# Moving a weight pool to the other end of SBUF, with the operand tiles below it, and splitting the recurrence scores into quarters

## The chip, the cores and the metric

One core of one Trainium2 chip runs the whole program. The metric is device time in microseconds (us) of one execution, lower is better. The median of three timed runs of the kernel before is 2441.2 us (2435.44 to 2445.77).

## What is computed

The input is 256 tokens of width 2048, float32. Three layers follow each other, and nearly all arithmetic is in dense products of those 256 tokens with weight matrices that are read once:

```python
# first block
u = rms_norm(h, mix_pre_g)
q, k, v, ca, cb, ga, gb = split(u @ w_in)                 # 2048 -> 9216
y_attn = neighbourhood_attention(q, k, v, rpb) @ w_attn_o
y_conv = conformer_conv(ca, cb, w_dw, b_dw, ln_g, ln_b, w_conv_o)
h = h + rms_norm((sigmoid(ga) * y_attn + sigmoid(gb) * y_conv) @ w_out, mix_post_g)
gate, up = split(rms_norm(h, ffn_pre_g) @ w_gate_up)      # 2048 -> 2 x 5632
h = h + rms_norm((silu(gate) * up) @ w_down, ffn_post_g)  # 5632 -> 2048
# second block, even layer
q, k, v, g_a, u, g_b = split(x @ w_in)                    # 2048 -> 6144
x = layer_norm(alpha * x + concat(stick_breaking(q, k, v) * silu(g_a), pool(u) * silu(g_b)) @ w_out)
# second block, odd layer: 32 heads of 64, products w_r w_k w_v w_g, two small lora products, and per head
sa = state @ (-kk_t)
state = state * w_t + sa * (kk_t * a_t) + v_t * k_t
o_t = state @ r_t
x = layer_norm(alpha * x + (norm(o) + bonus) * silu(g) @ w_o)
```

The recurrence is not stepped token by token. The kernel takes chunks of 64 tokens, and its scores are products within a chunk between two rows of keys, receptances and their decays ("gram" below).

## The kernel before

**Products.** Every float32 operand is kept as a high part and a remainder, both in the fp32r type, and a product is the sum of three matmuls: high by high, high by remainder, remainder by high. A weight piece of 256 rows by 512 columns is one DMA of 512 KB on SP's queue (`split_w`, L146) into `wraw`; ScalarE (ACT) copies it to `wh` (L149), VectorE (DVE) subtracts to get `wl` (L151). Four pieces of each are held in the pool "wts".

There are two forms of product. `ws` (weight-stationary, L168 to L170) loads a 128 by 128 block of the weights into TensorE (PE) and streams the 256 tokens of `x` past it; it serves outputs that are wanted with features on the partitions. `ts` (token-major, L187 to L189) loads a 128 by 128 block of `x` and streams 512 weight columns past it. In the trace's names the moving operand stands first: `acc<-xk,wh` is `ws`, `acc<-wh,xk` is `ts`. The `x` of a product lies in one of four kinds of tile: `xk` (a ring of 16 tiles, by far the most), `slab` (the mixer: attention output and convolution output, for w_attn_o and w_conv_o), `f` (the 44 row blocks of the gated FFN, for w_down), and `evm` (the merged tensor of the even layer, for its w_out). `xpool` tiles of the even layer share the `evm` slots and go through `ws`-like lines L846 to L848; the odd layer's small lora products are L1029 to L1031 and L1045 to L1047, with their weights `lh`, `ll` stationary and `lm`, `lx` moving.

**What sets the order.** Each engine runs its own list in order. PE's list interleaves the products with "background" pieces: `tick()` is called after each weight piece and releases one piece of queued work (transposes, attention heads, the recurrence). A tile pool hands out addresses when it is opened, from the bottom of SBUF upwards by default, and a pool closed gives them back.

**Start.** `mixer` calls `ahead(first_tile, 6, 0, ...)`: six blocks of 128 features (`x_piece`, 256 features each, L306) are read, transposed on PE (L246), scaled and split into `xk` (ACT L316, DVE L317) before the first product; the other ten come from the background. SP's queue takes the pieces in the order x0 w0 x1 w1 x2 w2 x3 x4 w3. ACT's first activation instruction needs a table load, which is placed ahead of it in ACT's list.

**Recurrence.** 16 units (4 groups of heads by 4 chunks) each run `gram` (L1360): per pair p, two matmuls, one on the upper 64 partitions of the operands and one on the lower 64, each with all 128 columns stationary and 128 moving, both float32 (each shows as two records, so 16 records a unit). `gmask` then zeroes what a score must not see, and later steps read 64-column parts of the result G.

Of the kernel before, what the change touches and what calls it, by code (L numbers as in the profile page):

```python
# [8 lines left out]
F32 = mybir.dt.float32  # L9
F32R = mybir.dt.float32r  # L10
# [27 lines left out]
class Mega:  # L38
    def __init__(self, ctx, tc, a, out):
        self.ctx, self.tc, self.nc, self.a, self.out = ctx, tc, tc.nc, a, out  # L40
        self.bg, self.loads, self.ready = [], deque(), deque()
        self.barrier = None
        self.cp = ctx.enter_context(tc.tile_pool(name="const", bufs=1))
        self.wp = ctx.enter_context(tc.tile_pool(name="wts", bufs=1))
        self.split_pool, self.depth = (self.wp, 4), 3
        self.xp = ctx.enter_context(tc.tile_pool(name="ring", bufs=16))
        self.sp = ctx.enter_context(tc.tile_pool(name="small", bufs=2))
        self.c1 = ExitStack()
        self.sp1 = self.c1.enter_context(tc.tile_pool(name="small1", bufs=1))
        self.pacc = ctx.enter_context(tc.tile_pool(name="pacc", bufs=4, space=bass.MemoryType.PSUM))  # L50
        self.paux = ctx.enter_context(tc.tile_pool(name="paux", bufs=4, space=bass.MemoryType.PSUM))
# [102 lines left out]

    def ws(self, W, col0, X, evac):

        nc = self.nc
        kt = self.a[W].shape[1] // P
        ps = [self.acc() for _ in range(4)]
        for k0 in range(0, kt, 2):  # L160
            wh, wl = self.next_w(W, col0, k0)
            for n in range(4):
                c = slice(n * P, n * P + P)
                o = ps[n][:, :T]
                for kk in range(2):
                    k = k0 + kk
                    x = X[k]
                    nc.tensor.matmul(o, wh[:, kk, c], x[:, 0], start=k == 0, stop=False)  # L168
                    nc.tensor.matmul(o, wh[:, kk, c], x[:, 1], start=False, stop=False)  # L169
                    nc.tensor.matmul(o, wl[:, kk, c], x[:, 0], start=False, stop=k == kt - 1)  # L170
                if k0 + 2 == kt:
                    evac(n, o)
            self.tick()
# [92 lines left out]
    def constants(self):  # L266
        nc, cp, a = self.nc, self.cp, self.a
        self.ident = cp.tile([P, P], F32, name="ident")
        nc.gpsimd.memset(self.ident, 1.0)
        nc.gpsimd.affine_select(out=self.ident, in_=self.ident, pattern=[[-1, P]], channel_multiplier=1,  # L270
                                base=0, compare_op=ALU.is_equal, fill=0.0)
        self.ones = cp.tile([P, P], F32, name="ones")
        nc.gpsimd.memset(self.ones, 1.0)
        self.mhalf = cp.tile([P, 16], F32, name="mhalf")
        nc.gpsimd.memset(self.mhalf, -0.5)

        src = a["vecs"]
        nblk = src.shape[0] // P
        self.vec = cp.tile([P, nblk * P], F32, name="vec")
        st = self.sp1.tile([P, nblk, P], F32, name="vst")  # L280

        def turn(b):
            ps = self.aux()
            nc.tensor.transpose(ps[:, :P], st[:, b], self.ident)
            nc.vector.tensor_copy(self.vec[:, b * P:b * P + P], ps[:, :P])

        def load():
            with self.tc.issue_after(self.paced[1].ins):
                nc.scalar.dma_start(out=st[:, 1:], in_=src[P:].rearrange("(b r) p -> r b p", r=P))

        nc.scalar.dma_start(out=st[:, 0], in_=src[0:P])
        turn(0)

        self.later = [load] + 4 * [lambda: None] + [lambda b=b: turn(b) for b in range(1, nblk)]
# [60 lines left out]
    def mixer(self):  # L355
        nc, a = self.nc, self.a
        ctx = ExitStack()
        pp = ctx.enter_context(self.tc.tile_pool(name="mix", bufs=1))
        W = "w_in"

        def slab(shape, dt=F32):
            return pp.tile(shape, dt, tag="slab", name="slab", bufs=6)

# [4 lines left out]
                self.x_piece(k // 2)  # L370

        def first_tile(k):
            if k % 2 == 0 and k < 6:
                self.x_piece(k // 2)
            x = self.to_fm(k, "mix_pre_g")
            if k % 2 and k < 6:
                with self.tc.issue_after(self.turned.ins):
                    self.fetch_w(k // 2 + 1)
            return x
        X = self.ahead(first_tile, 6, 0, fetch=piece)  # L380
        norm = {}

        def squares(c):
# [256 lines left out]
    def ffn(self, X, parts):  # L640
        nc, a = self.nc, self.a
        ctx = ExitStack()
        pp = ctx.enter_context(self.tc.tile_pool(name="ffn", bufs=1))
        W = "w_gate_up"
        r = self.rpow(self.ssq_total(parts), 2, 1.0 / D, 1e-6)
# [3 lines left out]
        def turn(gt):  # L649
# [12 lines left out]
            def halves(m):  # L662
                def go():
                    ps = st[m].rearrange("p (n t) -> p n t", n=2)
                    f = pp.tile([P, 2, 2, T], F32R, tag="f", name="f", bufs=FT // 2)
                    nc.scalar.activation(out=f[:, :, 0], in_=ps, func=AF.Copy)
                    nc.vector.tensor_tensor(out=f[:, :, 1], in0=ps, in1=f[:, :, 0].bitcast(F32), op=ALU.subtract)
                    F.extend(f[:, n] for n in range(2))
                return go
# [47 lines left out]
    def even(self, X):  # L717
        nc, a = self.nc, self.a
        ctx = ExitStack()
        pp = ctx.enter_context(self.tc.tile_pool(name="even", bufs=1))  # L720
        W = "ev_w_in_2"
        scale = 128.0 ** -0.5
# [75 lines left out]
        def pool_group(g):  # L798
# [13 lines left out]
            def means():  # L812
                for n in range(2):
                    d = pp.tile([P, T], F32, tag="pd", name="pd", bufs=2)
                    nc.vector.tensor_tensor(out=d, in0=st["sum"][:, n, 16:], in1=icnt[:, g], op=ALU.mult)
                    nc.vector.tensor_tensor(out=d, in0=d, in1=up[:, 2 * g + n, 16:], op=ALU.subtract)
                    x = pp.tile([P, 2, T], F32R, tag="evm", name="xpool", bufs=8)
                    self.split(x, d)
                    pooled[2 * g + n] = x
            return sums, means  # L820
# [37 lines left out]
        for i in range(2):  # L858
            def ev_ga(n, ps, i=i):
                t = pp.tile([P, T], F32, tag="gt", name="gt", bufs=2)  # L860
                nc.scalar.activation(out=t, in_=ps, func=AF.Silu)
                nc.vector.tensor_tensor(out=t, in0=t, in1=oa[:, 4 * i + n], op=ALU.mult)
                x = pp.tile([P, 2, T], F32R, tag="evm", name="evm", bufs=8)
                self.split(x, t)
                M[4 * i + n] = x
            self.ws(W, 3072 + 512 * i, X, ev_ga)
# [26 lines left out]
    def odd(self, normed):  # L893
# [411 lines left out]
        def bank(n=CH):  # L1305
            return self.aux()[:, :4 * n].rearrange("p (u s) -> p u s", s=n)
# [16 lines left out]
        def unit(j, c):  # L1323
# [31 lines left out]
            def gram():  # L1355
                ar, bk, G = st["ar"], st["bk"], st["G"]
                pss = [bank(P) for _ in HALF]
                for p in range(4):
                    for h2, hs in enumerate(HALF):
                        nc.tensor.matmul(pss[h2][:, p], bk[hs, p], ar[hs, p], start=True, stop=True)  # L1360
                for h2, ps in enumerate(pss):
                    nc.vector.tensor_tensor(out=G[:, h2], in0=ps, op=ALU.mult,
                                            in1=gmask[:, h2].unsqueeze(1).broadcast_to((P, 4, P)))
# [366 lines left out]
```

## Time and profile before

| | us |
|---|---|
| median of 3 runs | 2441.2 |
| the profiled execution's own time | 2436.61 |
| its span on the core | 2434.8 |
| PE busy within the span | 2372.7 |
| DVE busy | 1515.6 |
| ACT busy | 1214.4 |
| POOL busy | 223.4 |

The profiled execution lies 4.6 us under the median. Its time holds 1.8 us outside the span. The mean granted clock of TensorE is 0.991 of full speed. A PE matmul is pipelined: the "us" or "mean ns" of one reaches from its start to its modelled end and overlaps the next one, so what a stream of matmuls costs is read from the distance between starts (the pitch), either from two starts with the number of matmuls between them, or from the number of matmuls in a window that holds nothing else.

### The profile page before, as it was taken

What the parts mean: (1) busy time and instruction counts of PE and PEld (TensorE: products, weight loads), DVE (VectorE), ACT (ScalarE), POOL (GpSimd) and SP (SyncE); (2) the same over time, 40 slices, a digit from 0 to 9 for tenths busy, and PEclk for the clock granted to TensorE, in tenths of its full rate; (3) what the DMA queues carried; (4) which work ended last, traced back from release to release, by engine and by line L of the source; (5) the groups of instructions that cost most, each with busy time, mean ns of one, the idle gap of its engine ahead of it and who ended that gap; (6) DMA issues with size and microseconds to landing.
All of it is one profiled execution on the core that took longest, in us unless ns stands there. A gap on an engine that the chain in (4) does not pass through costs nothing.

```text
span 2434.8 us, 39170 instructions
## 1 busy us (share of the span) xinstructions
PE 2372.7 (97%) x15385; PEld 2072.3 (85%) x15385; DVE 1515.6 (62%) x2093; ACT 1214.4 (50%) x1937; POOL 223.4 (9%) x343
## 2 busy tenths in 40 slices
PE   8999999999999999999999999999999998999997
PEld 8998888788788888888888898999889996789975
DVE  5688888565654454454444544555587678885656
ACT  5433564444544444444344444564387765455662
POOL 0000200100000000000000000320000013145411
PEclk9999999999999999999999999999999999999998
DMA  7666656556566666666666556455666688866665
GB/s 230 196 185 192 175 170 189 160 185 203 160 191 190 190 190 185 191 191 190 193 194 191 168 184 190 149 164 182 196 189 194 185 238 232 220 169 157 149 169 135
DMA packets 287912, 451.18 MB, mean 185 GB/s; under 512 B 57903, under 2 KB 85103, under 8 KB 287727
## 3 DMA queue, kind: packets, MB, share of 16 engines
q1 hardware_dynamic: 263488, 428.50, 59.9%
q10 hardware_dynamic: 21167, 11.79, 1.8%
q0 software_dynamic: 3072, 8.39, 1.6%
q8 instruction: 121, 1.98, 0.3%
q14 instruction: 64, 0.52, 0.1%
HBM read 428.74 MB, written 17.77 MB: 183 GB/s over the span
## 4 chain that ended last, share of the span: by engine, by line
PE 78%; issue 7%; DVE 6%; DMA 4%; ACT 3%; POOL 1%; SPq 0%; ACTq 0%; DVEq 0%; POOLq 0%
PE acc L187 17%; PE acc L188 17%; PE acc L189 17%; PE acc L168 7%; PE acc L169 7%; PE acc L170 7%; DVE wl L151 2%; DMA wraw<-in_od_w_v 1%; ACT wh L149 1%; DMA wraw<-in_od_w_g 1%; DMA wraw<-in_od_w_k 0%; DMA inv<-md 0%; PE aux L246 0%; PE aux L659 0%; DVE xk L65 0%
## 5 line engine op out<-in xcount | busy, mean ns | idle before, releaser
L151 DVE TENSOR_TENSOR wl<-wraw,wh 128x1024 fp32r<-128x1024 f32 x762 | 935.1, 1228 | 752.8 <-ACT wh L149 750.0
L149 ACT ACTIVATE wh<-wraw 128x1024 fp32r<-128x1024 f32 x762 | 805.9, 1058 | 1004.4 <-PE acc L189 644.6
L187 PE MATMUL acc<-wh,xk 128*128 128x512 f32 x1520 | 599.6, 395 | 1.8 <-ACT kr L1226 1.3
L188 PE MATMUL acc<-wl,xk 128*128 128x512 f32 x1520 | 595.2, 392 | 5.4 <-DVE wl L151 5.3
L189 PE MATMUL acc<-wh,xk 128*128 128x512 f32 x1520 | 594.9, 391 | 0.0
L168 PE MATMUL acc<-xk,wh 128*128 128x256 f32 x1920 | 550.3, 288 | 0.5 <-ACT rr L1069 0.5
L169 PE MATMUL acc<-xk,wh 128*128 128x256 f32 x1920 | 544.5, 284 | 0.0
L170 PE MATMUL acc<-xk,wl 128*128 128x256 f32 x1920 | 540.8, 284 | 0.6 <-DVE wl L151 0.6
L168 PEld LDWEIGHTS acc<-xk,wh 128*128 128x128 f32 x1920 | 369.4, 193 | 4.4 <-ACT rr L1069 0.9
L169 PEld LDWEIGHTS acc<-xk,wh 128*128 128x128 f32 x1920 | 370.0, 193 | 0.4
L170 PEld LDWEIGHTS acc<-xk,wl 128*128 128x128 f32 x1920 | 367.5, 192 | 1.6 <-DVE wl L151 1.2
L188 PEld LDWEIGHTS acc<-wl,xk 128*128 128x128 f32 x1520 | 286.0, 188 | 65.3 <-DVE wl L151 7.5
L187 PEld LDWEIGHTS acc<-wh,xk 128*128 128x128 f32 x1520 | 285.9, 188 | 61.4 <-ACT kr L1226 1.5
L189 PEld LDWEIGHTS acc<-wh,xk 128*128 128x128 f32 x1520 | 286.1, 188 | 59.6
L187 PE MATMUL acc<-wh,f 128*128 128x512 f32 x352 | 139.1, 395 | 0.0
L188 PE MATMUL acc<-wl,f 128*128 128x512 f32 x352 | 138.9, 395 | 0.0
L189 PE MATMUL acc<-wh,f 128*128 128x512 f32 x352 | 138.9, 395 | 0.0
L427 DVE SCALAR_TENSOR_TENSOR slab<-zp,vec,slab 128x256 f32<-128x256 f32 x240 | 117.9, 491 | 4.2
L189 PEld LDWEIGHTS acc<-wh,f 128*128 128x128 f32 x352 | 66.3, 188 | 15.5
L187 PEld LDWEIGHTS acc<-wh,f 128*128 128x128 f32 x352 | 66.3, 188 | 15.5
L188 PEld LDWEIGHTS acc<-wl,f 128*128 128x128 f32 x352 | 66.3, 188 | 15.3
L725 POOL TENSOR_SCALAR_AFFINE_SELECT tri<-ones 128x128 f32<-128x128 f32 x1 | 0.3, 294 | 727.0 <-ACT junk L235 727.0
(318 smaller groups left out, 2149.1 us busy)
## 6 DMA issues: line engine op xcount, KB each, us to landing
wraw<-in_w_gate_up SPq DMA_DIRECT2D x176, 512.0 KB, 3.6
wraw<-in_w_in SPq DMA_DIRECT2D x144, 512.0 KB, 4.3
wraw<-in_ev_w_in SPq DMA_DIRECT2D x96, 512.0 KB, 3.6
wraw<-in_w_down SPq DMA_DIRECT2D x88, 512.0 KB, 4.7
wraw<-in_w_out SPq DMA_DIRECT2D x32, 512.0 KB, 4.2
wraw<-in_ev_w_out SPq DMA_DIRECT2D x32, 512.0 KB, 4.8
wraw<-in_od_w_r SPq DMA_DIRECT2D x32, 512.0 KB, 4.7
wraw<-in_od_w_k SPq DMA_DIRECT2D x32, 512.0 KB, 4.6
```

Of the source, the lines that this page charges most:

```text
L149: high = nc.scalar.activation(out=wh, in_=raw, func=AF.Copy)
L151: low = nc.vector.tensor_tensor(out=wl, in0=raw, in1=wh.bitcast(F32), op=ALU.subtract)
L168: nc.tensor.matmul(o, wh[:, kk, c], x[:, 0], start=k == 0, stop=False)
L169: nc.tensor.matmul(o, wh[:, kk, c], x[:, 1], start=False, stop=False)
L170: nc.tensor.matmul(o, wl[:, kk, c], x[:, 0], start=False, stop=k == kt - 1)
L187: nc.tensor.matmul(ps[t], x[:, 0, c], wh[:, kk], start=k == k1, stop=False)
L188: nc.tensor.matmul(ps[t], x[:, 0, c], wl[:, kk], start=False, stop=False)
L189: mm = nc.tensor.matmul(ps[t], x[:, 1, c], wh[:, kk], start=False, stop=k == k2 - 1)
L427: nc.vector.scalar_tensor_tensor(out=zc[:, n], in0=src, scalar=self.v1("w_dw", j * 8 + n), in1=zc[:, n], op0=ALU.mult, op1=ALU.add)
L725: nc.gpsimd.affine_select(out=tri, in_=self.ones, pattern=[[-1, P]], channel_multiplier=1, base=0, compare_op=ALU.is_ge, fill=0.0)
```

## The change

It has four parts.

1. **Pools.** The weight pool "wts" is opened at the right-hand side (the upper end) of SBUF. The slots of `slab`, `f` and of `evm` with `xpool` get pools of their own, "slabs", "gated" and "merged", opened first in their stage and so directly above the ring and the small pools, which themselves slide down by the size of the weight pool. Bytes per partition as both programs are built:

| tiles | before | after |
|---|---|---|
| weights (wraw, wh, wl) | 36544 to 85696 | 180192 to 229344 |
| xk ring | 85696 to 118464 | 36544 to 69312 |
| slab | 146176 to 195328 | 81792 to 130944 |
| f (22 tiles of 4096) | 139072 to 229184 | 81792 to 171904 |
| evm and xpool | 198464 to 214848 | 75072 to 91456 |
| lora weights lh | 186336 and up | between 133824 and 172048 |

   By the remainder of the start address modulo 256: weights and xk both 192 before, 224 and 192 after; f and evm 64, slab 0 before; f and slab 128, evm 64 after. In the last product of the kernel before (w_o), the second half of the weights lies at 182976 and up, remainder 192, moving past stationary xk.

2. **Start.** A small activation "warm" on a constant stands ahead of all others on ACT. Only four blocks are made before the first product; the transposes of the blocks after the fourth are placed behind the last product matmul written so far. SP's order becomes x0 w0 x1 w1 x2 w2 x3 w3 x4.

3. **Scores.** Each of gram's matmuls becomes two, with 64 stationary columns each; the four quarters of a pair go in the order (0,0), (1,1), (0,1), (1,0) of (row half, column half). 16 matmuls a unit in place of 8, with the same output.

4. **What moves along.** Other addresses decide which tile waits for which, so the scheduler's order differs at the border of FFN and even layer and within the recurrence; elsewhere the lists agree up to line numbers.

```diff
-        self.wp = ctx.enter_context(tc.tile_pool(name="wts", bufs=1))
+        self.wp = ctx.enter_context(tc.tile_pool(name="wts", bufs=1, side="right"))
...
-                    nc.tensor.matmul(o, wl[:, kk, c], x[:, 0], start=False, stop=k == kt - 1)
+                    self.mm = nc.tensor.matmul(o, wl[:, kk, c], x[:, 0], start=False, stop=k == kt - 1)
...
+        nc.scalar.activation(out=self.sp1.tile([P, 16], F32, name="warm"), in_=self.mhalf, func=AF.Copy)
...
+        lower = ctx.enter_context(self.tc.tile_pool(name="slabs", bufs=6))
         pp = ctx.enter_context(self.tc.tile_pool(name="mix", bufs=1))
...
-            return pp.tile(shape, dt, tag="slab", name="slab", bufs=6)
+            return lower.tile(shape, dt, tag="slab", name="slab")
...
         def first_tile(k):
-            if k % 2 == 0 and k < 6:
+            if k in (0, 2):
                 self.x_piece(k // 2)
-            x = self.to_fm(k, "mix_pre_g")
-            if k % 2 and k < 6:
+            with self.tc.issue_after(self.mm.ins) if k >= 4 else ExitStack():
+                x = self.to_fm(k, "mix_pre_g")
+            if k in (1, 3):
                 with self.tc.issue_after(self.turned.ins):
                     self.fetch_w(k // 2 + 1)
+            if k == 3:
+                self.x_piece(2)
             return x
-        X = self.ahead(first_tile, 6, 0, fetch=piece)
+        X = self.ahead(first_tile, 4, 0, fetch=piece)
...
+        lower = ctx.enter_context(self.tc.tile_pool(name="gated", bufs=FT // 2))
...
+        lower = ctx.enter_context(self.tc.tile_pool(name="merged", bufs=8))
...
                 for p in range(4):
-                    for h2, hs in enumerate(HALF):
-                        nc.tensor.matmul(pss[h2][:, p], bk[hs, p], ar[hs, p], start=True, stop=True)
+                    for h2, i in ((0, 0), (1, 1), (0, 1), (1, 0)):
+                        nc.tensor.matmul(pss[h2][HALF[i], p], bk[HALF[h2], p, col[i]], ar[HALF[h2], p],
+                                         start=True, stop=True)
```

ACT's list at the start of the program, before:

```order
L291 DMA vst<-in_vecs 128x128
L316 ACT_TABLE_LOAD
L316 ACTIVATE xk<-aux,vec 128x256 x2
L149 ACTIVATE wh<-wraw 128x1024
L316 ACTIVATE xk<-aux,vec 128x256 x2
```

and with the change (L319 is the old L316, L150 the old L149):

```order
L294 DMA vst<-in_vecs 128x128
L278 ACT_TABLE_LOAD
L278 ACTIVATE warm<-mhalf 128x16
L319 ACTIVATE xk<-aux,vec 128x256 x2
L150 ACTIVATE wh<-wraw 128x1024
```

The table load now belongs to an instruction that needs no transposed input; on PE the first row of transposes goes from x12 to x8 ahead of the first product.

PE's list around one gram of the recurrence, at 2127 us of the trace, before (L1412 transposes, L1417 the step that applies the inverse):

```order
L189 MATMUL acc<-wh,xk 128x512
L1412 MATMUL aux<-ident,unit 128x128 x4
L1417 MATMUL aux<-nv,Xt 64x64 x8
L1360 MATMUL aux<-unit 128x128 x8
L168 MATMUL acc<-xk,wh 128x256
```

and with the change:

```order
L190 MATMUL acc<-wh,xk 128x512
L1424 MATMUL aux<-ident,unit 128x128 x4
L1429 MATMUL aux<-nv,Xt 64x64 x8
L1371 MATMUL aux<-unit 64x128 x16
L169 MATMUL acc<-xk,wh 128x256
```

Nothing else moves there; eight matmuls with 128 stationary columns become sixteen with 64.

DVE's list at the border of FFN and even layer, before (L344 adds the FFN to h, L65 splits xk):

```order
L330 TENSOR_TENSOR fg<-acc,rowbc 128x512 x2
L239 TENSOR_REDUCE ssqt<-ssq 128x2
L151 TENSOR_TENSOR wl<-wraw,wh 128x1024
L344 SCALAR_TENSOR_TENSOR h<-fg,rpow,h 128x512 x4
L65 TENSOR_TENSOR xk<-aux,xk 128x256 x8
```

and with the change:

```order
L333 TENSOR_TENSOR fg<-acc,rowbc 128x512 x2
L240 TENSOR_REDUCE ssqt<-ssq 128x2
L347 SCALAR_TENSOR_TENSOR h<-fg,rpow,h 128x512 x4
L66 TENSOR_TENSOR xk<-aux,xk 128x256 x8
L347 SCALAR_TENSOR_TENSOR h<-fg,rpow,h 128x512 x4
```

One weight subtraction has left its place between the sum of squares and the update of h, and stands behind the xk splits.

## Rows read from the trace of the kernel before

**Rows 1.** The page: busy time of the engines, and the chain of work that ended last, by engine.

```profile
PE 2372.7 (97%) x15385; PEld 2072.3 (85%) x15385; DVE 1515.6 (62%) x2093; ACT 1214.4 (50%) x1937; POOL 223.4 (9%) x343
PE 78%; issue 7%; DVE 6%; DMA 4%; ACT 3%; POOL 1%; SPq 0%; ACTq 0%; DVEq 0%; POOLq 0%
```

**Rows 2.** Groups of PE instructions by line and shape over the whole span: count, busy us, mean ns of one, idle before.

```profile
L189 PE MATMUL acc<-wh,xk 128*128 128x512 f32 x1520 | 594.9, 391 | 0.0
L168 PE MATMUL acc<-xk,wh 128*128 128x256 f32 x1920 | 550.3, 288 | 0.5 <-ACT rr L1069 0.5
L189 PE MATMUL acc<-wh,f 128*128 128x512 f32 x352 | 138.9, 395 | 0.0
L189 PE MATMUL acc<-wh,slab 128*128 128x512 f32 x128 | 50.6, 395 | 0.0
L189 PE MATMUL acc<-wh,evm 128*128 128x512 f32 x64 | 25.2, 394 | 0.0
L1360 PE MATMUL aux<-unit 64*128 64x128 f32 x256 | 22.2, 290 | 5.1 <-DMA unit<-spill 2.5 <-ACT bt L1414 1.1 <-DVE unit L1362 1.0
```

**Rows 3.** What PE waited for: total us, times, longest.

```profile
PE aux L246 <- DVE h L344: 8.9, 2, 4.5
```

**Rows 4.** Timeline of PE, stretches of `ts` alone: start us, us of one. First xk (14 matmuls from the first row to the last), then f (14), then slab (12).

```profile
849.73 0.39 PE L188 MATMUL acc<-wl,xk 128*128 128x512 f32 x1
...
852.90 0.39 PE L187 MATMUL acc<-wh,xk 128*128 128x512 f32 x1
...
1199.71 0.40 PE L187 MATMUL acc<-wh,f 128*128 128x512 f32 x1
...
1202.96 0.40 PE L189 MATMUL acc<-wh,f 128*128 128x512 f32 x1
...
350.16 0.39 PE L188 MATMUL acc<-wl,slab 128*128 128x512 f32 x1
...
352.96 0.39 PE L188 MATMUL acc<-wl,slab 128*128 128x512 f32 x1
```

**Rows 5.** Busy time of PE in windows that hold one form alone, with the number of matmuls that touch the window, granted clock, DMA share and GB/s: `ws` with xk, `ts` with xk, `ts` with f, and `ts` with xk in the last product (weights at 182976 and up).

```profile
120.00:140.00 20.00, 20.00 (x169) 1.00 0.69 201
840.00:860.00 20.00, 20.00 (x90) 1.00 0.68 199
1150.00:1350.00 200.00, 200.00 (x862) 1.00 0.61 192
2380.00:2400.00 20.00, 20.00 (x90) 1.00 0.81 198
```

**Rows 6.** Timeline of PE, 256 moving columns: `ws` with xk (18 matmuls), the xpool products (13), the lora products (5).

```profile
129.72 0.28 PE L170 MATMUL acc<-xk,wl 128*128 128x256 f32 x1
...
131.88 0.28 PE L170 MATMUL acc<-xk,wl 128*128 128x256 f32 x1
...
1629.39 0.28 PE L846 MATMUL acc<-xpool,wh 128*128 128x256 f32 x1
...
1630.94 0.28 PE L847 MATMUL acc<-xpool,wh 128*128 128x256 f32 x1
...
1837.53 0.28 PE L1045 MATMUL aux<-lx,lh 96*128 96x256 f32 x1
...
1838.12 0.28 PE L1047 MATMUL aux<-lx,ll 96*128 96x256 f32 x1
```

**Rows 7.** Timeline of all engines at the start.

```profile
4.98 1.28 ACT L316 ACT_TABLE_LOAD   x1 [4.98 <-DVE vec L285]
...
6.28 0.84 ACT L316 ACTIVATE xk<-aux,vec 128x256 fp32r<-128x256 f32 x2
...
7.01 1.05 ACT L149 ACTIVATE wh<-wraw 128x1024 fp32r<-128x1024 f32 x1
...
7.11 1.12 PE L246 MATMUL aux<-ident,h 128*128 128x128 f32 x4 [1.68 <-DMA h<-in_x]
...
9.28 1.09 PE L246 MATMUL aux<-ident,h 128*128 128x128 f32 x4 [1.06 <-DMA h<-in_x]
...
10.02 0.56 PE L168 MATMUL acc<-xk,wh 128*128 128x256 f32 x1
```

**Rows 8.** Timeline of PE around gram: three units of 16 records, each with the row that follows it.

```profile
2127.43 1.16 PE L1360 MATMUL aux<-unit 64*128 64x128 f32 x16
2128.52 0.39 PE L168 MATMUL acc<-xk,wh 128*128 128x256 f32 x1
...
2220.22 1.88 PE L1360 MATMUL aux<-unit 64*128 64x128 f32 x16 [0.43 <-DVE Z L1419]
2222.03 0.39 PE L168 MATMUL acc<-xk,wh 128*128 128x256 f32 x1
...
2301.42 1.16 PE L1360 MATMUL aux<-unit 64*128 64x128 f32 x16
2302.43 0.40 PE L1504 MATMUL aux<-ident,h 64*128 64x64 f32 x4
```

**Rows 9.** Timeline at the border of FFN and even layer, DVE and PE.

```profile
1375.23 1.23 DVE L151 TENSOR_TENSOR wl<-wraw,wh 128x1024 fp32r<-128x1024 f32 x1 [0.19 <-ACT wh L149]
...
1377.05 2.74 DVE L344 SCALAR_TENSOR_TENSOR h<-fg,rpow,h 128x512 f32<-128x512 f32 x4 [0.59 <-POOL rpow L215]
...
1377.95 1.90 PE L246 MATMUL aux<-ident,h 128*128 128x128 f32 x8 [4.48 <-DVE h L344]
```

More of the change, by code (lines that the diff above doesn't have):

```diff
@@ L664, in go @@
                     ps = st[m].rearrange("p (n t) -> p n t", n=2)
-                    f = pp.tile([P, 2, 2, T], F32R, tag="f", name="f", bufs=FT // 2)
+                    f = lower.tile([P, 2, 2, T], F32R, tag="f", name="f")
                     nc.scalar.activation(out=f[:, :, 0], in_=ps, func=AF.Copy)
@@ L816, in means @@
                     nc.vector.tensor_tensor(out=d, in0=d, in1=up[:, 2 * g + n, 16:], op=ALU.subtract)
-                    x = pp.tile([P, 2, T], F32R, tag="evm", name="xpool", bufs=8)
+                    x = lower.tile([P, 2, T], F32R, tag="evm", name="xpool")
                     self.split(x, d)
@@ L862, in ev_ga @@
                 nc.vector.tensor_tensor(out=t, in0=t, in1=oa[:, 4 * i + n], op=ALU.mult)
-                x = pp.tile([P, 2, T], F32R, tag="evm", name="evm", bufs=8)
+                x = lower.tile([P, 2, T], F32R, tag="evm", name="evm")
                 self.split(x, t)
```

## The prediction

> **What bounds the kernel now.** I read the page's busy times and chain first [rows 1]: PE is busy 97 % of the span and carries 78 % of the chain that ended last, DVE 6 %, DMA 4 %. So a change pays only where it shortens PE's own stream or one of the few waits of PE. The groups by line [rows 2] say what the stream is: 3 x 1520 `ts` matmuls on xk, 3 x 352 on f, 3 x 128 on slab, 3 x 64 on evm (6192 together) and 3 x 1920 = 5760 `ws` matmuls on xk. Their mean durations overlap, so I took the pitch from starts. `ts` on xk: 3.17 us for 14, 226.4 ns each; on f 3.25 us for 14, 232.1 ns; on slab 2.80 us for 12, 233.3 ns [rows 4]. Windows agree [rows 5]: a window that counts n matmuls holds n less those in flight at its edge (389 / 227, about 1.7), which gives 226.5 ns for xk and 232.5 for f; for `ws` (2.3 in flight) 120.0. The granted clock is 1.00 in all four windows. Same instruction, same clock, same DVE and DMA work in kind, and yet an f, slab or evm matmul costs 5.6 to 6.8 ns more than an xk one. What differs is where the stationary tile lies: xk ends at 118464 of SBUF, the others begin at 139072.
>
> **The change, part by part.** The sum is made against the profiled execution, 2436.6 us; the median stands 4.6 above it, so I add 4.6 at the end.
>
> *Slab, f, evm.* If a low stationary tile is what makes xk quick, then the tiles that come down gain. All 384 slab matmuls (now below 130944): 384 x 6.8 = 2.6 us. Evm, below 91456: 192 x 5.6 = 1.1 us (its mean duration is f's within 1 ns, so I give it f's pitch [rows 2]). Of f's 22 tiles, 12 lie below 131072; the trace leaves the border between 118464 and 139072, so 9 to 14 tiles are possible: 1056 x 12/22 x 5.6 = 3.2 us. Together **-6.9 us**. The bounds are 0 (the address is not the cause) and -9.6 (all of f gains, 5.9 us, as it would if lying below the weights were what counts).
>
> *`ts` on xk.* The ring goes down to 36544 to 69312, the moving weights up to 180192. A low stationary xk against high moving weights is shown once: the last product, 226.5 ns [rows 5]. I take **0**. The other bound is the loss in the first rival below.
>
> *`ws`.* Now the stationary weights are high and the moving xk low. No row shows that pair. The nearest are xpool, low weights against a high moving tile, 1.55 us for 13, 119.2 ns, and the lora products, both high, 0.59 us for 5, 118.0 ns; `ws` on xk now takes 2.16 us for 18, 120.0 [rows 6]. So at 256 columns a distant or high operand has cost nothing. I take **0**, by the row it is nearest to in what moves (the 120.0 of xk), with -0.8 x 5760 = -4.6 us as the good end by xpool. The bad end is f's penalty carried over to a high stationary weight block: 5.6 x 5760 = +32 us.
>
> *Start.* Today ACT loads its table only when the first transposed input is ready, 1.28 us [rows 7]; "warm" puts that load into idle time before 4.98. The xk and wh activations behind it then run about 1.3 us earlier. PE has its second set of transposes from 7.11, as x1 lands, to 8.23; it now waits a further 1.06 us for x2 and transposes four more before the first product at 10.02. With eight transposes ahead, the first product can start at about 8.2 if wh and xk are ready: wh, begun at 7.01, would begin at about 5.8 unless its DMA is later. That is up to 1.8 us; the four transposes (some 1.1 us at that stage) are not saved but done behind. What is late next is the weights' arrival, and x3 comes one piece later on SP's queue, behind w3, with nothing queued behind it but x4 and the weights after. I take **-1.5**, bounds 0 and -1.8.
>
> *Scores.* 16 units occupy PE for 22.2 us [rows 2], 1.39 each; the well-packed ones take 1.16, with 1.01 to 1.09 until PE's next start, and one takes 1.88 [rows 8]. Twice as many matmuls with half the stationary columns: if the four quarters run together, each quarter streams as many columns as each half does now, and the unit keeps its length; all that can come back is the untidy units' excess, 22.2 - 16 x 1.16 = 3.6 us. If only two run together, a unit streams twice as long: the 1.16 less the 0.29 of one record [rows 2] is streaming, so +0.87 x 16 = +14 us. I take **-1.0**: most units are packed already. The quarters of one row half share its moving rows, which no row of this trace does on 64-row tiles.
>
> The Trainium skill bears on this term: "TensorEngine Tiling (Array Packing)", Key Properties, has tiles operate independently, which would give the first case; its Restrictions say that column tiling disables the fast weight load, and "TensorE: Matmul & The Clock Gate", Part 3, that a weight load overlaps running matmuls only when its row group differs, which speak for the second. By the first the sum stays as above, by the second it is about 14 us higher; no run here shows either on four quarters.
>
> *Border of FFN and even layer, recurrence order.* The wl subtraction that leaves its place ran 1375.23 to 1376.46, under POOL's rpow, and the update of h waited for rpow until 1377.05 [rows 9]; PE's 4.5 us wait [rows 3] therefore stays. Behind the xk splits it holds up only the third weight piece. I take **0**, bounds 0 and +1.2 (its duration, if that piece is needed at once). In the recurrence the lists are reshuffled around waits that stay; 0, give or take 2.
>
> **Sum:** -6.9 - 1.5 - 1.0 = -9.4; 2436.6 - 9.4 + 4.6 = **2431.8**, say 2432.
>
> **The rivals.**
>
> *The quick state needs the two operands in step, and the change breaks it (slower).* Wherever the pitch is 226.5 or 120.0, stationary and moving tiles begin at the same remainder modulo 256: xk and weights, both 192, and the last product, xk 192 with weights at 192. Slab (0), f and evm (64) against 192 are the slow ones. That explains the rows as well as low against high does. With the change weights stand at 224, xk at 192, slab and f at 128, evm at 64: nothing agrees. Then f, slab and evm gain nothing, and 4560 xk matmuls lose the difference, 4 ns by the mean durations (391 against 395 [rows 2]) to 5.6 by pitch: 18 to 26 us; I take 18, since a mean over all of them holds those that are out of step already. `ws` out of step would, by xpool, run 0.8 ns shorter: -4.6. With start and scores: 18 - 4.6 - 2.5 = +10.9, that is **2452**. It decides from the first xk stretch: at 228.5 ns or more the change is a loss. Against it: no row has an offset as small as 32 bytes.
>
> *Placement moves nothing.* Slab, f and evm stay slow at their new places and xk stays quick: 2436.6 - 2.5 + 4.6 = **2439**. The Trainium skill, "SBUF — State Buffer", section on the two separate sides, says that PE never waits on anyone at SBUF, by which placement would be neutral; the 5.6 ns between xk and f in rows 4 and 5 are not explained by it, since they stand between instructions that differ in their tile alone.
>
> *Two quarters at a time.* The forecast with +14 in place of -1: 2432 + 15 = **2447**.
>
> *`ws` gains too,* as xpool: 2432 - 4.6 = **2427**. *`ws` loses* f's penalty: 2432 + 32 = **2464**.
>
> **How the numbers follow.** Forecast 0.40 (its own range 2426 to 2436, from the terms of f, start and scores); operands out of step 0.20; placement neutral 0.17; two quarters 0.10; `ws` gains 0.08; `ws` loses 0.05. Range **2420 to 2458**: it leaves out `ws` losing, the worst of the first rival (2460 at 26 us) and the best ends together (2431.8 less 2.7 for all of f, 2.6 for the scores, 4.6 for `ws`, 2422, and a little for the recurrence), about 0.15. Half a per cent, 12 us, is about what a measurement of this kernel can tell from no change: faster is below 2429, slower above 2453.4. Faster: 0.4 of the forecast's spread, nearly all of `ws` gains, a little of neutral, 0.27. Slower: half of the first rival, `ws` losing, and some of two quarters, 0.19. Same: 0.54.
>
> **What would show it.** Mean duration of `ts` on slab and evm at 389 to 391 and their pitch at 227, f at 227 for its early tiles and 232 for the late ones: the region step. Xk's pitch at 232 and durations at 395: the first rival. `ws` pitch at 120.0, 119.2 or 125: the `ws` cases. First product at 8.2: start. A unit of gram at 1.0 to 1.2 against 1.9: the scores. The forecast is wrong if xk leaves 226.5, if slab stays at 233, or if a unit of gram doubles.

## The result and the profile after

The kernel is slower by about half a per cent: 2452.5 us against 2436.5, medians of seven runs each on one chip, ratio 1.0057 with a 95 % interval of 1.0044 to 1.0070. The profiled execution has a span of 2450.8 us, 16.0 above the 2434.8 of before, at a mean granted clock of 0.992 against 0.991. The 2441.2 us that the prediction's sum was raised to is the median of the first three of these seven runs of the kernel before; the median of all seven lies at the profiled execution, so the 4.6 us that the prediction added was scatter.

Page after: busy times and the chain, to set beside [rows 1].

```profile
PE 2389.8 (98%) x15641; PEld 2058.8 (84%) x15641; DVE 1515.7 (62%) x2093; ACT 1214.5 (50%) x1938; POOL 223.5 (9%) x343
PE 79%; issue 7%; DVE 6%; DMA 3%; ACT 3%; POOL 1%; SPq 0%; ACTq 0%; DVEq 0%; POOLq 0%
```

DVE, ACT and POOL are as before to 0.1 us. PE has 256 matmul records more and 17.1 us more of busy time, about the 16.0 that the span grew by. So the loss is in PE's own stream, not in waits. Groups of PE by line and shape say where; first those of before that [rows 2] did not have.

```profile
L187 PE MATMUL acc<-wh,xk 128*128 128x512 f32 x1520 | 599.6, 395 | 1.8 <-ACT kr L1226 1.3 <-ACT wh L149 0.4
L188 PE MATMUL acc<-wl,xk 128*128 128x512 f32 x1520 | 595.2, 392 | 5.4 <-DVE wl L151 5.3
L169 PE MATMUL acc<-xk,wh 128*128 128x256 f32 x1920 | 544.5, 284 | 0.0
L170 PE MATMUL acc<-xk,wl 128*128 128x256 f32 x1920 | 540.8, 284 | 0.6 <-DVE wl L151 0.6
```

And those of the kernel after.

```profile
L188 PE MATMUL acc<-wh,xk 128*128 128x512 f32 x1520 | 608.2, 401 | 2.1 <-ACT kr L1236 1.6 <-ACT wh L150 0.6
L189 PE MATMUL acc<-wl,xk 128*128 128x512 f32 x1520 | 604.0, 397 | 5.3 <-DVE wl L152 5.3
L190 PE MATMUL acc<-wh,xk 128*128 128x512 f32 x1520 | 603.2, 397 | 0.0
L169 PE MATMUL acc<-xk,wh 128*128 128x256 f32 x1920 | 547.3, 287 | 0.9 <-ACT rr L1079 0.4 <-ACT gate L1546 0.2 <-ACT xk L319 0.2
L170 PE MATMUL acc<-xk,wh 128*128 128x256 f32 x1920 | 541.4, 283 | 1.2 <-DVE xk L320 1.2
L171 PE MATMUL acc<-xk,wl 128*128 128x256 f32 x1920 | 537.9, 283 | 0.4 <-DVE wl L152 0.4
L190 PE MATMUL acc<-wh,f 128*128 128x512 f32 x352 | 138.8, 394 | 0.0
L1371 PE MATMUL aux<-unit 64*64 64x128 f32 x512 | 20.9, 274 | 4.4 <-DMA unit<-spill 1.8 <-DVE unit L1374 1.3 <-DVE Z L1431 0.8
```

The three lines of a form overlap one another, so their sum is more than the time that PE spent on them (1789.7 us for 4560 matmuls is 392 ns each, at a pitch of 227). The overlap is much the same in both kernels, so the difference of the sums can be used. `ts` on xk: 599.6 + 595.2 + 594.9 = 1789.7 before, 1815.4 after, **+25.7**, or 5.6 ns a matmul. `ws`: 550.3 + 544.5 + 540.8 = 1635.6 before, 1626.6 after, **-9.0**, or 1.6 ns. f, slab and evm, three lines each, moved by +0.4, -0.1 and +0.4, **+0.7** together. Gram: -1.3. The sum is +16.1, against a span that grew by 16.0. Taken over all pairs of neighbours of one form in the two traces, interruptions and stretches at the lower granted clock left out, the mean pitch agrees: `ts` on xk went from 227.2 to 233.1 ns, `ws` from 121.4 to 120.0.

The timeline of PE in the same stretches as [rows 4] and [rows 6] (start us, us of one): xk (12 matmuls from first row to last), f (14), slab (12), and `ws` on xk (19).

```profile
850.97 0.40 PE L189 MATMUL acc<-wl,xk 128*128 128x512 f32 x1
...
853.77 0.40 PE L189 MATMUL acc<-wl,xk 128*128 128x512 f32 x1
...
1199.62 0.39 PE L190 MATMUL acc<-wh,f 128*128 128x512 f32 x1
...
1202.89 0.39 PE L189 MATMUL acc<-wl,f 128*128 128x512 f32 x1
...
350.19 0.39 PE L188 MATMUL acc<-wh,slab 128*128 128x512 f32 x1
...
352.98 0.39 PE L188 MATMUL acc<-wh,slab 128*128 128x512 f32 x1
...
129.74 0.28 PE L169 MATMUL acc<-xk,wh 128*128 128x256 f32 x1
...
131.98 0.28 PE L170 MATMUL acc<-xk,wh 128*128 128x256 f32 x1
```

From starts: xk 2.80 / 12 = 233.3 ns (226.4 before), f 3.27 / 14 = 233.6 (232.1), slab 2.79 / 12 = 232.5 (233.3), `ws` 2.24 / 19 = 117.9 (120.0 before). The tiles that came down gained nothing, and xk joined them. The granted clock is 1.00 in these stretches in both kernels. The same kernel holds the counter-case in its last product, with stationary xk at remainder 192 throughout: first with weights from the moved pool (remainder 224), then with the second half of the weights, in another pool at 133824 (remainder 192).

```profile
2403.81 0.39 PE L189 MATMUL acc<-wl,xk 128*128 128x512 f32 x1
...
2405.91 0.40 PE L189 MATMUL acc<-wl,xk 128*128 128x512 f32 x1
...
2409.12 0.39 PE L188 MATMUL acc<-wh,xk 128*128 128x512 f32 x1
...
2411.84 0.39 PE L188 MATMUL acc<-wh,xk 128*128 128x512 f32 x1
```

2.10 us for 9 is 233.3 ns, 2.72 for 12 is 226.7.

### The profile page after: what moved, and what is told of

Same layout as the page of the kernel before. It is cut to its first block, busy times and chain, and to the rows that moved or that the text cites. A ratio compares the mean times of both kernels' runs of the same rounds, so it can differ in the third digit from the quotient of the medians.

```text
span 2450.8 us, 39682 instructions
## 1 busy us (share of the span) xinstructions
PE 2389.8 (98%) x15641; PEld 2058.8 (84%) x15641; DVE 1515.7 (62%) x2093; ACT 1214.5 (50%) x1938; POOL 223.5 (9%) x343
## 4 chain that ended last, share of the span: by engine, by line
PE 79%; issue 7%; DVE 6%; DMA 3%; ACT 3%; POOL 1%; SPq 0%; ACTq 0%; DVEq 0%; POOLq 0%
PE acc L188 18%; PE acc L189 18%; PE acc L190 18%; PE acc L169 7%; PE acc L170 7%; PE acc L171 7%; DMA wraw<-in_od_w_v 2%; DVE wl L152 2%; ACT wh L150 1%; DMA wraw<-in_od_w_k 0%; DVE inv L1269 0%; DVE inv L1267 0%; PE aux L668 0%; PE aux L247 0%; DVE xk L66 0%
## 5 line engine op out<-in xcount | busy, mean ns | idle before, releaser
L150 ACT ACTIVATE wh<-wraw 128x1024 fp32r<-128x1024 f32 x762 | 805.5, 1058 | 1020.6 <-PE acc L190 696.6
L188 PE MATMUL acc<-wh,xk 128*128 128x512 f32 x1520 | 608.2, 401 | 2.1 <-ACT kr L1236 1.6
L189 PE MATMUL acc<-wl,xk 128*128 128x512 f32 x1520 | 604.0, 397 | 5.3 <-DVE wl L152 5.3
L190 PE MATMUL acc<-wh,xk 128*128 128x512 f32 x1520 | 603.2, 397 | 0.0
L169 PEld LDWEIGHTS acc<-xk,wh 128*128 128x128 f32 x1920 | 363.6, 190 | 5.8 <-ACT rr L1079 0.9
L170 PEld LDWEIGHTS acc<-xk,wh 128*128 128x128 f32 x1920 | 364.4, 190 | 1.8 <-DVE xk L320 1.6
L171 PEld LDWEIGHTS acc<-xk,wl 128*128 128x128 f32 x1920 | 362.0, 189 | 1.6 <-DVE wl L152 1.0
L435 DVE SCALAR_TENSOR_TENSOR slab<-zp,vec,slab 128x256 f32<-128x256 f32 x240 | 117.3, 489 | 4.2
L190 PEld LDWEIGHTS acc<-wh,f 128*128 128x128 f32 x352 | 66.1, 188 | 17.1
```

Of the source, the lines that this page charges most:

```text
L150: high = nc.scalar.activation(out=wh, in_=raw, func=AF.Copy)
L171: self.mm = nc.tensor.matmul(o, wl[:, kk, c], x[:, 0], start=False, stop=k == kt - 1)
L188: nc.tensor.matmul(ps[t], x[:, 0, c], wh[:, kk], start=k == k1, stop=False)
L189: nc.tensor.matmul(ps[t], x[:, 0, c], wl[:, kk], start=False, stop=False)
L190: mm = nc.tensor.matmul(ps[t], x[:, 1, c], wh[:, kk], start=False, stop=k == k2 - 1)
L435: nc.vector.scalar_tensor_tensor(out=zc[:, n], in0=src, scalar=self.v1("w_dw", j * 8 + n), in1=zc[:, n], op0=ALU.mult, op1=ALU.add)
```

## The experiments

Two readings stood against each other. The region reading: where the stationary tile lies decides. The step reading (the first rival): the remainder modulo 256 of weights less x decides; "offset" below is that number (0 for xk in the kernel before, 32 in the kernel after). Each experiment is compared with runs of the kernel before on its own chip.

| run | edit | us | before | ratio (95 %) |
|---|---|---|---|---|
| e1_step32 | after, weights down 32 bytes | 2429.5 | 2437.8 | 0.9965 (0.9949 to 0.9981) |
| e2_all_step | e1, with slab, f, evm in step | 2427.5 | 2437.2 | 0.9958 (0.9943 to 0.9973) |
| e3_start_scores | before, with start and scores | 2436.2 | 2437.2 | 0.9998 (0.9989 to 1.0008) |
| e_place | after, without start and scores | 2455.0 | 2437.2 | 1.0067 (1.0050 to 1.0083) |
| e4_xk64 | e2, xk at offset 64 | 2418.2 | 2437.9 | 0.9915 (0.9900 to 0.9931) |
| e5_before32 | before, ring up 32 bytes | 2452.6 | 2437.9 | 1.0058 (1.0043 to 1.0074) |
| e6_before_step | before, slab, f, evm in step | 2431.6 | 2437.9 | 0.9966 (0.9954 to 0.9979) |

**map1: the pitch by itself.** Rows of 48 matmuls on zeros in one large tile, with the places of the two operands set by hand; nothing of the model is computed.

> This kernel does none of the model: it fills SBUF with zeros and runs 50 rows of 48 matmuls each, in the form of ts (128 stationary columns, 512 moving) and of ws (128 stationary, 256 moving), with no other engine at work; each row has its own byte addresses of x and weights. In step theory (start of moving and stationary tile agree modulo 256): the pitch of ts is 226.7 ns at offset 0 and 256 and 512, and 230 to 235 ns at 32, 64, 96, 128 and 160; it is the same at low and at high addresses; ws 120.0 at offset 0 and 118 to 119.5 elsewhere. Region theory (the weights' or the stationary tile's place decides): 226.7 for all 14 offsets with both tiles low, 231 to 234 with x at 146176 or above, or with weights at 194496 and above. Neither (other engines' traffic decides): 226.7 throughout.

Timeline rows of map1: six `ts` rows, then two `ws` rows. The pitch is the us less the last matmul (0.39; 0.28 for `ws`), over the count less one.

```profile
42.38 10.82 PE L62 MATMUL acc<-big 128*128 128x512 f32 x47
...
86.54 11.36 PE L66 MATMUL acc<-big 128*128 128x512 f32 x48
...
288.24 11.08 PE L91 MATMUL acc<-big 128*128 128x512 f32 x48
...
277.04 11.36 PE L90 MATMUL acc<-big 128*128 128x512 f32 x48
...
332.78 11.06 PE L96 MATMUL acc<-big 128*128 128x512 f32 x48
...
321.58 11.37 PE L95 MATMUL acc<-big 128*128 128x512 f32 x48
...
197.82 5.91 PE L76 MATMUL acc<-big 128*128 128x256 f32 x48
...
231.81 5.61 PE L82 MATMUL acc<-big 128*128 128x256 f32 x48
```

The first two are offset 0 and 32: 10.43 / 46 = 226.7 and 10.97 / 47 = 233.4. The next pair has low x and high weights, at offset 0 (about 227) and at 32, with the remainders of the kernel after (233.4). The third pair has x high, at offset 0 (227) and where slab stood before (233.6). Five more rows at offset 0, with remainders 0, 64, 192 and 224 common to both operands, had 226.7 to 227.5. So high or low is worth nothing, and the offset decides; the traffic of other engines, the third reading, falls too, since none is at work here. `ts` at 64 had 229, a little under the range foretold. `ws` goes the other way, and further than foretold: offset 0 gives 119.8, offset 64 113.4, the best of its rows.

**e1: put the weights in step.** A 32-byte tile ahead of the weight pool brings it from remainder 224 to 192.

```diff
+        pad = ctx.enter_context(tc.tile_pool(name="pad", bufs=1, side="right"))
+        nc = self.nc
+        nc.gpsimd.memset(pad.tile([P, 8], F32, name="pad"), 0.0)
         self.wp = ctx.enter_context(tc.tile_pool(name="wts", bufs=1, side="right"))
```

> The changed kernel with a 32-byte tile above the weight pool, so that the weights start 32 bytes lower, at 180160, and agree with the xk ring modulo 256 (192 both); nothing else. In step theory: ts on xk returns to 226 to 228 ns and ws to 120.0; slab, f and evm stay at 231 to 235, since they stand at 128 and 64; the whole is 2430 to 2436 us, 17 to 22 under the changed kernel and a little under the kernel before (start and scores). Region theory: xk stays at 232 to 233 with the weights still at the upper end, and the whole within 3 us of 2452.

PE's timeline, xk (12 matmuls).

```profile
850.72 0.39 PE L191 MATMUL acc<-wh,xk 128*128 128x512 f32 x1
...
853.44 0.39 PE L191 MATMUL acc<-wh,xk 128*128 128x512 f32 x1
```

2.72 / 12 = 226.7 ns: xk is quick again, from 32 bytes, with the weights still at the upper end. The loss has turned into a gain of 0.35 %. One part was not as foretold: slab and f, at offset 64 here, were not left at 231 to 235. Their busy sums fell by 1.4 and 3.8 us against the kernel after, and the mean pitch of f over its starts is 228.9.

**e5: take the kernel before out of step.** The converse, with none of the change in it. The ring moves up, so xk's offset becomes 224, which is 32 bytes the other way.

```diff
+        pad = ctx.enter_context(tc.tile_pool(name="pad", bufs=1))
+        tc.nc.gpsimd.memset(pad.tile([P, 8], F32, name="pad"), 0.0)
         self.xp = ctx.enter_context(tc.tile_pool(name="ring", bufs=16))
```

> The kernel before with a 32-byte tile between the weight pool and the xk ring: no pool moves, no other part of the change is in it, only the remainders part (weights 192, xk 224; slab 32, f and evm 96). Step theory: ts on xk 233.3 (+6 x 4560 = +27), ws 116.6 to 117.8 (-2.2 to -3.4 x 5760 = -13 to -20), slab, f and evm within 1 ns of before: +7 to +15, so 2444 to 2452. If the place at the upper end were what costs, no change: 2437 within 3.

PE's timeline: xk (12), then `ws` (16).

```profile
850.77 0.40 PE L189 MATMUL acc<-wh,xk 128*128 128x512 f32 x1
...
853.57 0.40 PE L189 MATMUL acc<-wh,xk 128*128 128x512 f32 x1
...
129.64 0.28 PE L171 MATMUL acc<-xk,wh 128*128 128x256 f32 x1
...
131.51 0.28 PE L172 MATMUL acc<-xk,wl 128*128 128x256 f32 x1
```

233.3 ns and 1.87 / 16 = 116.9. Thirty-two bytes alone give the change's ratio, 1.0058 against 1.0057, just above the 2444 to 2452 that were foretold.

**e_place: placement without the rest.** Start and scores set back to those of before.

```diff
-        X = self.ahead(first_tile, 4, 0, fetch=piece)
+        X = self.ahead(first_tile, 6, 0, fetch=piece)
...
-                    for h2, i in ((0, 0), (1, 1), (0, 1), (1, 0)):
+                    for h2, hs in enumerate(HALF):
```

> The changed kernel without its start and split scores: the placement alone. Step theory: xk at offset 32, ts on xk 233 (6.6 x 4560 = +30 us at most), ws 118.3 (-1.7 x 5760 = -9.8), so about +16 to +20 on the kernel before: 2453 to 2458, 3 to 4 over the changed kernel. If the loss came from the new start or the split scores, it would be within 3 us of the kernel before.

1.0067: the placement carries the whole loss.

**e3: start and scores alone.**

```diff
+        nc.scalar.activation(out=self.aux()[:, :16], in_=self.mhalf, func=AF.Copy)
...
-        X = self.ahead(first_tile, 6, 0, fetch=piece)
+        X = self.ahead(first_tile, 4, 0, fetch=piece)
...
-                    for h2, hs in enumerate(HALF):
+                    for h2, i in ((0, 0), (1, 1), (0, 1), (1, 0)):
```

> The kernel before with the start and the split scores of the change, and all tiles where they were (warm writes to a PSUM tile so that it takes no room in SBUF). Both theories: start -1.5 to -2.0, scores -1 to -2, so 2434 to 2435, 2.5 to 4 us under the kernel before; were two quarters at a time the rule, it would be some 12 us over it.

0.9998: anything from -2.7 to +1.9 us, so this run can tell neither the gain foretold nor a small loss from nothing. Timeline of e3's start, to set beside [rows 7].

```profile
8.74 0.56 PE L168 MATMUL acc<-xk,wh 128*128 128x256 f32 x1
...
17.89 1.06 ACT L149 ACTIVATE wh<-wraw 128x1024 fp32r<-128x1024 f32 x1 [1.39 <-DMA wraw<-in_w_in]
...
25.11 0.39 PE L169 MATMUL acc<-xk,wh 128*128 128x256 f32 x1 [0.86 <-DVE xk L319]
```

The first product comes 1.28 us sooner than the 10.02 of before. By 18 us ACT waits 1.39 us for a weight piece to land, and PE waits for the splits of blocks that are now made behind the products. Matched one by one, the `ws` matmuls of e3 lead those of before by 1.29 us up to the 72nd (20.67 us in before) and by 0.56 at the 96th (23.97); the 192nd (36.79) comes 1.03 us later than in before. The kernel after set against e_place, which has its addresses but not its start, shows the same: 2.4 us ahead at the first product, 0.4 behind at the 192nd. So in these profiles, one of each kernel, the lead is not only lost, the start ends up to 1 us behind: the transposes that were put off are done among the products, and PE waits for their splits.

**e6: before, with only slab, f and evm brought in step,** still at the upper end.

```diff
+        step = ctx.enter_context(self.tc.tile_pool(name="step", bufs=1))
+        nc.gpsimd.memset(step.tile([P, 48], F32, name="step"), 0.0)
         pp = ctx.enter_context(self.tc.tile_pool(name="mix", bufs=1))
```

(and 128 bytes ahead of the pools "ffn" and "even").

> The kernel before with unused tiles ahead of slab (192 bytes), f (128) and evm (128), so that they start at 192 as the weights do; they stay in the upper half of SBUF (139200 and above). Step theory: ts on them falls to 226.7: 1056 x 5.7 + 384 x 6.5 + 192 x 5.7 ns = 9.6 us, so about 2427.5. Region theory (stationary tile high costs): no change, 2437 within 3.

PE's timeline on a late f tile (13 matmuls), then the wait for the spilled operand in the recurrence (total us, times, longest; 2.5 before).

```profile
1339.83 0.39 PE L189 MATMUL acc<-wh,f 128*128 128x512 f32 x1
...
1342.78 0.39 PE L187 MATMUL acc<-wh,f 128*128 128x512 f32 x1
```

```profile
PE aux L1366 <- DMA unit<-spill: 4.8, 1, 4.8
```

2.95 / 13 = 226.9 ns on tiles above 139200, where the region reading has the slow ones. The three forms' busy sums fell by 5.9, 2.3 and 1.0, together 9.2 us where 9.6 were foretold; the median fell by 6.3 and the profiled span by 4.7. What took the rest is not shown. Two things differ between the profiles: the wait shown is 2.3 us longer, and the mean granted clock is 0.989 against 0.991 of before, which over 2430 us can be worth up to 5 us (an estimate: the difference times the span). The clock fell to 1.2 GHz behind PE's longer waits: in before, PE stood idle for 4.48 us up to 1377.95 [rows 9] and had half the clock from 1378.1 to 1381.5. The wait by itself is no sign of a PE that comes too soon: e_place, 23 us slower than e6, has one of 4.8 us too.

**e2: the placement after, all in step.** e1 with 64 unused bytes ahead of "slabs" and "gated" and 128 ahead of "merged".

```diff
+        step = ctx.enter_context(self.tc.tile_pool(name="step", bufs=1))
+        nc.gpsimd.memset(step.tile([P, 16], F32, name="step"), 0.0)
         lower = ctx.enter_context(self.tc.tile_pool(name="slabs", bufs=6))
```

> The run with the weights moved down by 32 bytes, and also small unused tiles ahead of the slab, f and evm pools, so that all of them start at remainder 192 as xk and the weights do. Step theory: ts on slab, f and evm falls to 226.7; by the first map slab and f stood at offset 64 (229.0) and evm at 128 (232.4 to 233.4), so 1440 x 2.3 + 192 x 6 ns = 4.5 us less than e1_step32: about 2425. Region theory with only low stationary tiles quick: the late f tiles (above 131072) stay at 232 and the whole falls by under 1 us.

Timeline, a late f tile (14 matmuls).

```profile
1339.67 0.39 PE L193 MATMUL acc<-wh,f 128*128 128x512 f32 x1
...
1342.85 0.39 PE L192 MATMUL acc<-wl,f 128*128 128x512 f32 x1
```

3.18 / 14 = 227.1 ns. f was at offset 64 in e1, a mild one by map1 (229.0), and had little left to gain. The busy sums of f, slab and evm fell by 4.3 us against e1, 4.5 foretold. The median of 2427.5 is only 2 us lower, on another chip, and the intervals of e1 and e2 overlap, so the whole does not show the gain; the profiled granted clock was 0.990 here and 0.992 in e1.

**e4: give `ws` its best offset.** By map1 offset 64 costs `ts` 2.3 ns and spares `ws` 6.7. The constant "mhalf" moves out from under the ring, which puts xk at remainder 128 against weights at 192; slab, f and evm stay in step.

```diff
+        self.hp = ctx.enter_context(tc.tile_pool(name="half", bufs=1))
...
-        self.mhalf = cp.tile([P, 16], F32, name="mhalf")
+        self.mhalf = self.hp.tile([P, 16], F32, name="mhalf")
```

> The run with every operand at the weights' remainder, with one more edit: the 64-byte constant mhalf is taken from below the xk ring to above it, so that the weights stand 64 bytes after xk modulo 256 (192 against 128), while slab, f and evm stay in step with the weights. By both maps, at offset 64 ws takes 113.3 ns in place of 120.0 and ts 228.9 in place of 226.7: -6.7 x 5760 + 2.2 x 4560 = -38.6 + 10.0 = -28.6 us, so 2427.5 - 28.6 = about 2399. If the maps held only for engines at rest, or if the interruptions by transposes keep ws from reaching 113, ws would stay at 117 to 120 and the whole would be 2420 to 2437.

PE's timeline, two stretches of `ws` (15 matmuls, then 44).

```profile
109.80 0.28 PE L174 MATMUL acc<-xk,wh 128*128 128x256 f32 x1
...
111.50 0.28 PE L174 MATMUL acc<-xk,wh 128*128 128x256 f32 x1
...
127.78 0.28 PE L175 MATMUL acc<-xk,wl 128*128 128x256 f32 x1
...
132.96 0.28 PE L174 MATMUL acc<-xk,wh 128*128 128x256 f32 x1
```

The first is 1.70 / 15 = 113.3 ns, the second 5.18 / 44 = 117.7: at one offset `ws` falls into either of two rhythms. Against e2 its busy sum fell by 26.8 us, short of 6.7 x 5760 = 38.6; `ts` on xk rose by 9.8, as 2.3 x 4560 = 10.5 would have it. The forecast of 2399 was missed by 19 us: 12 of them are the slower rhythm of `ws`, and of the net 17 us in the sums only 9 reached the median, for reasons that were not followed. It is the fastest version here, 0.9915 of before.

**map2: a finer map.** All offsets in steps of 4, so that most rows have another row before them than in map1; again no model.

> Again none of the model: rows of 48 matmuls on zeros with the weights' start set off from that of x by 0, 4, 8, ... 252 bytes, first 64 rows of ts, then 64 of ws. Step theory: ts 226.7 ns only near offset 0 (0 and 240 in the first map) and 229 to 238 elsewhere; ws 120.0 at 0, 113 at 64, 115 to 118 elsewhere; each row is the same as in the first map. If the pitch depended on what ran before the row, rows that are in both maps would differ by more than 1 ns.

`ts` was at 226.7 at offset 0 alone, and between 229 and 240 elsewhere; `ws` had 113.3 to 113.6 at 52, 64, 76 and 88. But offset 240 gave `ts` 236.6 where map1 had 226.7, and `ws` at 32 gave 6.29 / 47 = 133.8 in this row of map2's timeline, where map1 had 118.3. Three other rows that are in both maps differ by 1 to 3 ns (`ts` at 48, `ws` at 96 and 224).

```profile
805.07 6.57 PE L134 MATMUL acc<-big 128*128 128x256 f32 x48
```

So the offset does not fix the rhythm by itself.

**map3: what runs before.** Eight targets, each entered from eight offsets; no model.

> None of the model: 64 pairs of rows of 48 matmuls on zeros; the first row of a pair runs at an entry offset (0, 8, 20 or 28, 32, 64, 96, 128, 192), the second at the offset that is looked at: 0, 240, 64, 32 for ts, then 0, 64, 32, 96 for ws. If the offset alone sets the pitch, the eight second rows of one offset agree within 0.5 ns. If the offset only sets which rhythms can stand and the rhythm before chooses: ts at 0 is 226.7 eight times, ts at 240 is 226.7 some times and about 236.5 others, ws at 64 is 113.3 some times and 117.8 others (as in the run with xk at 64), ws at 32 is 118.3 some times and 133.3 others.

From starts, `ts` at 0 gave 226.7 to 227.5 and `ts` at 32 233.2 to 233.4, eight times each, and `ws` at 0 and 32 held 119.9 to 120.0 and 118.3. `ts` at 240 gave 236.5 to 236.7 seven times and 233.3 once; the 226.7 of map1 did not come. `ts` at 64 gave 229 seven times, and 233.3 when entered from 8. `ws` at 96 gave 120.0 four times, 117.3 twice and 118.7 to 118.8 twice. `ws` at 64, entered from 0 and from 8:

```profile
851.93 5.82 PE L143 MATMUL acc<-big 128*128 128x256 f32 x48
...
863.14 5.61 PE L145 MATMUL acc<-big 128*128 128x256 f32 x48
```

5.54 / 47 = 117.8, then 113.4, and 113.3 from the six other entries. The offset decides which rhythms can stand, and what ran just before can choose among them. The two offsets of the question, 0 and 32, had one each in every entry of this run; the 133.8 did not come again.

## Why the prediction was wrong

**What bounds the kernel** held: PE carries 79 % of the chain, and the span moved by what PE's stream moved.

**The step that failed** is the reading of the quick `ts`: "What differs is where the stationary tile lies". It picked one of two differences that fit every row of before. Out of it came both wrong terms: -6.9 for slab, f and evm (measured +0.7), and "I take **0**" for `ts` on xk (measured +25.7). The row called a low xk against high moving weights was in step as well, so it could not tell the readings apart. Rival 1 stated the mechanism and gave 2452; the median is 2452.5. I discounted it because no row had an offset as small as 32 bytes; e5 is that row (32 bytes the other way), at +14.6 us.

**The rival's sizes** were too small, and its 2452 is in part luck. It forecast +10.9 us; the change cost 16.0. The 4.6 us added for the median of three runs made up nearly all of the difference, and the seven runs do not have it. Its xk price of 18 was the gap of 4 ns between the mean durations of xk and f. The 26 at its other end, from the pitch, was right (25.7). Mean durations of two kinds of tile do not compare: in the kernel after, xk's stand at 397 to 401 and f's at 394 although both run at a pitch of 233; one line of xk before and after does compare (391 and 397). For `ws` the -4.6 rested on xpool's 0.8 ns; it took 1.6 a matmul, -9.0 measured, beyond the good end given. The 118.0 of the lora products came from two rows rounded to 10 ns; the trace's own starts give 119.4.

**Placement neutral** falls with e1 and e5. The Trainium skill's "SBUF — State Buffer", section "SBUF: two separate sides", has PE never waiting on anyone there, by which 32 bytes would cost nothing. In e5 the ring and what lies above it moved up by 32 bytes and nothing else changed in PE's work, and its `ts` pitch is 233.3 against 226.4. Whether the delay arises in SBUF or in PE's own fetching no run shows, so the measurement contradicts the neutral reading and not necessarily the sentence.

**Start** came as told in the kernel after (first product at 7.99, foretold 8.2), but its -1.5 was not kept: in e3's profile the lead had turned into 1.0 us behind by 37 us, outside the bounds of 0 and -1.8. The sum had the four transposes done behind at next to no price. **Scores:** the units did not double.

```profile
2125.36 1.10 PE L1371 MATMUL aux<-unit 64*64 64x128 f32 x32
2126.40 0.50 PE L188 MATMUL acc<-wh,xk 128*128 128x512 f32 x1
```

In this timeline of the kernel after, a unit of 32 records keeps PE 1.04 us until its next start, as 16 records did before [rows 8]: the four quarters do run together. The Trainium skill's "TensorEngine Tiling (Array Packing)", Key Properties, has tiles operate independently, and the trace agrees. The group is 1.3 us less busy, about the -1.0 taken. e3 cannot tell start and scores together (-2.5 foretold) from nothing.

**Border** was taken at 0, with PE's wait of 4.5 us staying. It became 3.57 (POOL's row of before first, then POOL's and PE's of after):

```profile
1375.41 1.60 POOL L215 TENSOR_TENSOR rpow<-rpow,mhalf 128x2 f32<-128x2 f32 x1
...
1394.46 0.70 POOL L216 TENSOR_TENSOR rpow<-rpow,mhalf 128x2 f32<-128x2 f32 x1
...
1396.09 1.74 PE L247 MATMUL aux<-ident,h 128*128 128x128 f32 x8 [3.57 <-DVE h L347]
```

The subtraction did not lie free under rpow, the power of the norm: beside it this POOL instruction took 1.60 us, without it 0.70. At the border of mixer and FFN the subtraction kept its place, and there rpow takes 1.60 and PE waits 4.5 us in both kernels. So the new order gave back 0.9 us, outside the bounds of 0 and +1.2.

What is shown: the offset of the two start addresses modulo 256 moves the pitch both ways (e1, e5, e6), and the place in SBUF does not (map1, e6). What stays open: by which part of the chip, and by what rule a stream of matmuls settles in one of several rhythms.

## What to carry to other kernels

When a pool is moved or a small tile added below one, compare the start addresses modulo 256 of the two matmul operands before and after; here 32 bytes were worth 0.6 %. Read a matmul stream's cost from starts, or from one line's busy time in both kernels, not from the mean durations of two kinds of tile; and where two differences explain the same rows, build the placement that parts them before trusting either. Work that is put off, as the four transposes are, is still to be paid: follow a lead past the point where it was won. And a gain in the busy sums need not reach the whole: of 9.2 us in e6 the median kept 6.3.

## What the runs showed of the hardware

The two forms of product want different offsets: `ts` is quickest at 0 (226.7 ns for 512 columns), `ws` at 64 (113.3 for 256, against 120.0 at 0), a pitch that it also took at 76 and 88 in map2 and in three rows at 192 in map3. At the granted 2.4 GHz the pitches 226.7, 233.3 and 240.0 of `ts` are 544, 560 and 576 clocks, and 113.3 and 120.0 of `ws` are 272 and 288, all multiples of 16. But these are means over a stretch, and others (229, 231.6, 117.8, 118.3) are not such multiples. In step, single distances between starts are even (226 or 227 ns for `ts` on xk in before). Out of step they are not: the xk stretch of the kernel after goes through 235, 233, 235 and 230 ns, so its 233.3 is a mean of uneven distances. One offset can hold two pitches (117.8 and 113.3 in map3), chosen by what ran before. And POOL's power of two columns took 1.60 us with a DVE subtraction of two SBUF tiles beside it, 0.70 without.
